# The weight-block sums of a seven-product projection, computed by GpSimd instead of VectorE

## The chip, the cores and the metric

The kernel runs on one core of a Trainium2 chip. A core has five engines that run their own instruction streams and wait for each other through semaphores: TensorE (PE, matrix products; PEld is its weight load), VectorE (DVE, elementwise), ScalarE (ACT, functions, copies and casts), GpSimd (POOL, elementwise, here almost idle) and SyncE (SP, which issues transfers). The metric is the device time of one execution in microseconds; a shorter time is better. Before the change the median of 3 runs is 1056.26 us (1055.57 to 1057.36).

## The reference

One inference step of a decoder trunk of two layers, for a prompt of 512 tokens and 8 sample tokens, 1024 wide. Layer 0 is a recurrent branch beside a state-space branch. Layer 1, where the change lies, is this, cut to what matters:

```python
def layer_c(h, p, s_c, lb, norm_w, w_in, c_norm_w, w_out, ple_w, ple_g):
    u = rmsnorm(h, norm_w) @ w_in
    q, fx, v, gate = jnp.split(u, [HK_C, 2 * HK_C, 2 * HK_C + D_C], axis=-1)
    g = jnp.logaddexp(jnp.log(lb), jnp.log1p(-lb) + jax.nn.log_sigmoid(fx))
    k = (1.0 - lb) * jax.nn.sigmoid(-fx)
    o, new_c = hgrn2_scan(q * DK_C ** -0.5, k, v, g, s_c)      # 16 heads of 128 x 128, by chunks
    o = o * lax.rsqrt(jnp.mean(o * o, axis=-1, keepdims=True) + EPS)
    o = o.reshape(Bsz, L, D_C) * c_norm_w * jax.nn.silu(gate)
    h = h + o.astype(h.dtype) @ w_out
    return per_layer_embed(h, p, ple_w, ple_g), new_c
```

The projection `u` has the four parts q, f (`fx`), v and gate (g), each 1024 x 2048 weights for 16 heads.

## The kernel before, in words

All 520 tokens (512 of the prompt, 8 samples) stay on the chip, features on the partitions, tokens on the free axis. Every float32 weight is loaded raw into `wraw` (two buffers of 128x2048) and split into a rounded part (`whir`, made by ACT) and the rest (`wlor` = raw minus rounded part, made by DVE); a product is then three matmuls, rounded weight by both parts of the activations and the rest by the rounded activations. In layer 1 the splits go through a ring with room for four half-size pieces (128x512) of either part, so a piece can be prepared at most a few products ahead of TensorE.

Layer 1 (`layer1_fast`) works through eight pairs of heads. For the first pair, f and v are plain projections. For the other seven pairs, `strassen` computes f and then v of both heads with seven block products instead of eight. A pair's weight group is cut into four blocks of 128x512: a11 and a12 (the two halves of the 1024 inputs, first head), a21 and a22 (the same, second head); the tokens are cut into two halves of 260. Four sums of weight blocks are needed: s3 = a11 + a21, then a21 = a21 + a22 in place, s2 = a21 + a11, and later a12 = a12 + s2 in place. The seven products take, in the order of the code, a11, s2, s3, a12 as loaded, the new a21, the new a12 and a22, each after its own split (`split_half`). DVE adds the products together from PSUM. s2 and s3 live in two buffers (tag `sgt`); v's s3 takes the buffer of f's s3 and v's s2 that of f's s2, so each can be written only when f's has been used up. Each product is 12 matmuls of 260 columns.

Around them, each pair also runs `decay` (a scan along the prompt per head), `samples` (the 8 samples' states: 30 small DVE updates of 128x128 and 18 scalings on ACT or DVE, and one matmul per head named `os`), and `head`, twice: `A`, `kt`, `kv` on PE, the chunk states S (`l1d`) on DVE, seven matmuls named `o`, the root mean square of the output with its power on POOL (`at__1738<-at__1738,nhalf`, `pow`), and the transpose `ot`.

The order of the work is not the order of the code. A planner (`Plan.order`) takes every recorded operation with its data dependences, a price per operation from a table (`COST`: a DVE `tensor_tensor` of n columns 0.067 + n/960 us, a POOL one 0.21 + n/480 us) and a due time, and plays the five engines through; each engine's instructions are then issued in the sequence that came out, and on the chip each engine keeps to it. A piece of work that the plan thinks ready earlier is therefore put earlier in the stream of every engine that takes part. Operations that may run on ACT or DVE (`copy`, `scaled`) go to the one that is free first in the plan. PE's `os` and `o` blocks are put behind their inputs with a spare of 0.6 us. The plan's prices do not know of one engine's access holding up another's. Nearly all instructions are recorded by `issue`, so they all carry line L520 in the profile and are told apart by their tiles.

Of the kernel before, what the change touches and what calls it, by code (L numbers as in the profile page):

```python
# [21 lines left out]
MUL, ADD, SUB, MAX, MIN = ALU.mult, ALU.add, ALU.subtract, ALU.max, ALU.min  # L22
# [187 lines left out]
class Plan:  # L210
# [31 lines left out]
    @contextmanager  # L242
    def side(self, start=0.0, rate=0.0, pinned=False):

        keep = self.shift, self.rate, self.pinned
        self.shift, self.rate, self.pinned = start, rate, pinned
        yield
        self.shift, self.rate, self.pinned = keep
# [15 lines left out]
    @contextmanager  # L264
    def block(self, main=False):

        self.open = Op(self, self.pos + self.shift, 0)
        self.open.forms["pe"] = [[], 0.0, None]
        self.open.main = main
        self.open.ins, self.open.outs = [], []  # L270
        yield
        op, self.open = self.open, None
        op.forms["pe"][1] /= 2400.0
        self.add(op, op.ins, op.outs)
# [266 lines left out]
def hybrid_decode_step_kernel(ctx: ExitStack, tc: tile.TileContext, I, O, mode="both"):  # L541
# [19 lines left out]
    act, dve, pool, pe, sp = (Engine(plans, k) for k in ("act", "dve", "pool", "pe", "sp"))  # L561
    side, block = (lambda *a, **k: plans[-1].side(*a, **k)), (lambda *a: plans[-1].block(*a))

    def new(pool_, shape, tag, name, bufs=1, dt=F32):
        return plans[-1].tile(pool_, shape, dt, tag, name, bufs, {"psm": PSUM, "psa": PSUM, "drp": DRAM}.get(pool_, SBUF))
# [4 lines left out]
    def mmps(name):  # L570
        return new("psm", [128, 2, 512], "mm", name, 2)

    def grab(name):

        return new("psa", [128, 512], "ax", name)
# [10 lines left out]
    def tt(out, a, b, op, eng=dve):  # L586
        eng.tensor_tensor(out=out, in0=a, in1=b, op=op)
# [13 lines left out]
    def copy(out, in_):  # L601

        plans[-1].record(("act", "copy", (out, in_), {}), ("dve", "tensor_copy", (out, in_), {}))
# [25 lines left out]
    def load_group(g):  # L629
        ap, k0, kk, c, w = groups[g]  # L630
        r = new("wp", [128, 2048], "raw", f"wraw{g}", 2)
        v = r[:, :kk * w].rearrange("p (k c) -> p k c", k=kk)
        with side(*((plans[-1].shift, 0.0, True) if plans[-1].pinned else (-LOAD_AHEAD,))):
            sp.dma_start(out=v, in_=ap[k0 * 128:(k0 + kk) * 128, c:c + w].rearrange("(k p) c -> p k c", p=128))
        raw_of[g] = v
# [9 lines left out]
    def split_half(v):  # L645

        hv, lv = (r.rearrange("p (k c) -> p k c", k=4) for r in ring_space(1))
        with side(-SPLIT_AHEAD):
            act.copy(hv, v)
            tt(lv, v, hv.bitcast(F32), SUB)  # L650
        return hv, lv
# [959 lines left out]
    def layer1_fast():  # L1611
# [93 lines left out]
        def strassen(pr, names):  # L1705

            pss, n = [], 0

            def product(u, x):
                nonlocal n  # L1710

                i = n % 6
                if i % 3 == 2:
                    out = grab(f"sg{pr}_{n}")[:, :HN]
                else:
                    if i < 2:
                        pss[i:] = [mmps(f"sm{pr}_{n}")]
                    out = pss[i % 3][:, i // 3, :HN]
                n += 1
                hw, lw = u  # L1720
                for k in range(4):
                    with block(True):
                        for i, (w, b) in enumerate(((hw, x[0]), (hw, x[1]), (lw, x[0]))):
                            pe.matmul(out, lhsT=w[:, k], rhs=b[:, k], start=(k == 0 and i == 0), stop=(k == 3 and i == 2))
                    plans[-1].pos += 0.334
                return out

            def steps(nm):
                e, e1 = 2 * pr, 2 * pr + 1
                start, done = (start_f, done_f) if nm == "f" else (start_v, done_v)  # L1730
                o0, o1 = start(e), start(e1)
                l0, r0, l1, r1 = o0[:, :HN], o0[:, HN:], o1[:, :HN], o1[:, HN:]
                g = units[sec[f"{nm}{pr}"]][0]
                if g not in raw_of:
                    load_group(g)
                v = raw_of[g]
                a11, a12, a21, a22 = v[:, :4, :128], v[:, 4:, :128], v[:, :4, 128:], v[:, 4:, 128:]
                s2, s3 = (new("cst", [128, N], "sgt", f"{nm}{pr}s{i}", 2)[:, :512].rearrange("p (k c) -> p k c", k=4)
                          for i in range(2))
                w = split_half(a11)  # L1740
                with side(-SPLIT_AHEAD):
                    tt(s3, a11, a21, ADD)
                    tt(a21, a21, a22, ADD)
                    tt(s2, a21, a11, ADD)
                p1 = product(w, x11)
                copy(l0, p1)
                p6 = product(split_half(s2), u2)
                tt(r0, l0, p6, ADD)
                p7 = product(split_half(s3), t3)
                tt(l1, p7, r0, SUB)  # L1750
                w = split_half(a12)
                with side(-SPLIT_AHEAD):
                    tt(a12, a12, s2, ADD)
                p2 = product(w, x21)
                tt(l0, l0, p2, ADD)
                p5 = product(split_half(a21), u1)
                tt(r1, l1, p5, SUB)
                tt(r0, r0, p5, ADD)
                p3 = product(split_half(a12), x22)
                tt(r0, r0, p3, ADD)  # L1760
                done(e)
                p4 = product(split_half(a22), u4)
                tt(l1, l1, p4, ADD)
                done(e1)

            for nm in names:
                steps(nm)
# [497 lines left out]
```

## Time and profile before

| | before |
|---|---|
| median of 3 runs | 1056.26 us |
| the profiled execution's own time | 1052.58 us |
| its span (first to last instruction) | 1050.9 us |
| busy share PE / DVE / ACT / POOL | 97% / 79% / 60% / 13% |
| granted TensorE clock | 0.994 |

The profiled execution lies 3.7 us under the median of the runs. Layer 1's pairs take about 450 us to 950 us of the span. A row of a group gives busy time, mean duration and the idle time before; a row of the timeline gives start, duration, engine and operation, the output tile before the arrow and inputs after it; consecutive DVE instructions overlap a little in the record, so that a 128x512 sum that lasts 0.68 us is followed by the next after 0.60 us.

### The profile page before, as it was taken

How to read it: one execution, taken by the hardware profiler on the slowest of the kernel's cores; microseconds unless marked ns; L12 is line 12 of the kernel's file. 1: busy time of each engine (PE TensorE's matmuls, PEld its weight loads, DVE VectorE, ACT ScalarE, POOL GpSimd, SP SyncE). 2: the span in 40 equal slices, each digit the busy share in tenths (PEclk: the TensorE clock that was granted, in tenths of full speed). 3: DMA queues.
4: the chain of work that ended last, by engine and by line, in shares of the span. 5: the costliest groups of instructions: out<-in, count | busy, mean ns of one | idle time of the engine just before them, and what ended most of it. 6: DMA issues, size and time to landing. Idle time of an engine off the chain costs nothing.

```text
span 1050.9 us, 21517 instructions
## 1 busy us (share of the span) xinstructions
PE 1023.1 (97%) x8427; PEld 1000.0 (95%) x8427; DVE 832.6 (79%) x1705; ACT 630.8 (60%) x1482; POOL 139.4 (13%) x241
## 2 busy tenths in 40 slices
PE   9989899999999999999999999999999999999995
PEld 8989899899999999999999999999999999999995
DVE  6789788998996656697989759698598979868853
ACT  6588876654673222365676726678268685764553
POOL 4635854100000000001000000001000000100000
PEclk9999999999999999999999999999999999999998
DMA  9712254336586223553353433433434443553311
GB/s 285 246 30 92 81 166 141 122 110 191 188 257 213 89 98 117 153 203 90 98 149 109 142 91 108 139 100 113 122 90 139 124 116 111 137 180 121 121 41 45
DMA packets 129957, 138.45 MB, mean 132 GB/s; under 512 B 13704, under 2 KB 111128, under 8 KB 129832
## 3 DMA queue, kind: packets, MB, share of 16 engines
q1 hardware_dynamic: 129464, 136.64, 42.6%
q8 instruction: 68, 1.11, 0.4%
q10 hardware_dynamic: 160, 0.30, 0.1%
q14 instruction: 41, 0.34, 0.1%
q0 software_dynamic: 224, 0.06, 0.0%
HBM read 111.71 MB, written 25.44 MB: 131 GB/s over the span
## 4 chain that ended last, share of the span: by engine, by line
PE 73%; DVE 10%; DMA 6%; ACT 4%; POOL 3%; issue 2%; SPq 0%; POOLq 0%; ACTq 0%; DVEq 0%
PE o L520 10%; PE sm L520 9%; PE q L520 9%; PE pg L520 9%; PE g L520 8%; PE ob L520 4%; PE sg L520 4%; PE xbc L520 2%; PE ax L520 2%; DVE wlo L520 2%; PE oa L520 2%; PE pl L520 2%; PE z L520 1%; DMA smp<-in_state_b_ssm_dram 1%; POOL csm L520 1%
## 5 line engine op out<-in xcount | busy, mean ns | idle before, releaser
L520 ACT CAST whir<-wraw 128x512 fp32r<-128x512 f32 (+1 forms) x121 | 96.3, 798 | 83.9 <-PE o L520 40.6
L520 DVE TENSOR_TENSOR wlor<-wraw,whir 128x512 fp32r<-128x512 f32 (+1 forms) x121 | 109.6, 910 | 12.5 <-ACT whir L520 12.1
L520 ACT CAST whi<-wraw 128x1024 fp32r<-128x1024 f32 (+1 forms) x56 | 57.8, 1032 | 48.6 <-PE ob L520 34.5
L520 POOL TENSOR_TENSOR at__1738<-at__1738,nhalf 128x4 f32<-128x4 f32 (+1 forms) x24 | 22.6, 942 | 461.5 <-DVE at__1738 L520 455.5
L520 DVE TENSOR_TENSOR wlo<-wraw,whi 128x1024 fp32r<-128x1024 f32 (+1 forms) x64 | 77.3, 1208 | 8.0 <-ACT whi L520 7.4
L520 PE MATMUL o<-ohl,whir 128*128 128x260 f32 x512 | 83.0, 284 | 0.0
L520 PEld LDWEIGHTS o<-ohl,whir 128*128 128x128 f32 x512 | 70.0, 188 | 0.9 <-issue 0.6
L520 PE MATMUL g<-xh,whir 128*128 128x260 f32 x256 | 54.6, 294 | 1.1 <-DVE l1a L520 1.1
L520 PE MATMUL q<-xh,whir 128*128 128x260 f32 x256 | 53.2, 289 | 0.0
L520 PE MATMUL q<-xh,wlor 128*128 128x260 f32 x256 | 51.5, 283 | 0.0
L520 PE MATMUL q<-xl,whir 128*128 128x260 f32 x256 | 51.4, 282 | 0.0
L520 PE MATMUL g<-xl,whir 128*128 128x260 f32 x256 | 51.4, 282 | 0.0
L520 PE MATMUL g<-xh,wlor 128*128 128x260 f32 x256 | 51.4, 282 | 0.0
L520 PE MATMUL o<-ohl,wlor 128*128 128x260 f32 x256 | 51.4, 282 | 0.0
L520 DVE TENSOR_TENSOR h<-h,o 128x520 f32<-128x520 f32 x40 | 27.8, 694 | 26.2 <-PE o L520 25.9
L515 ACT ACT_TABLE_LOAD x36 | 46.2, 1283 | 0.6
L520 PE MATMUL sm<-uh,whir 128*128 128x260 f32 x140 | 40.4, 289 | 1.8 <-DVE l1a L520 1.6
L520 PE MATMUL sm<-xh,whir 128*128 128x260 f32 x140 | 41.4, 296 | 0.0
L520 PEld LDWEIGHTS g<-xh,whir 128*128 128x128 f32 x256 | 39.2, 189 | 2.2 <-DVE l1a L520 1.3
L520 PE MATMUL sm<-xh,wlor 128*128 128x260 f32 x140 | 39.6, 283 | 0.3 <-DVE wlor L520 0.3
L520 PE MATMUL xbc<-xnh,whi 128*128 128x260 f32 x192 | 39.7, 289 | 0.0
L520 PE MATMUL sm<-xl,whir 128*128 128x260 f32 x140 | 39.6, 283 | 0.0
(609 smaller groups left out, 3594.2 us busy)
## 6 DMA issues: line engine op xcount, KB each, us to landing
wraw<-in_c_w_in_dram SPq DMA_DIRECT2D x32, 1024.0 KB
wraw<-in_ab_w_in_dram SPq DMA_DIRECT2D x15, 1024.0 KB
wraw<-in_ab_w_out_dram SPq DMA_DIRECT2D x8, 1024.0 KB
wraw<-in_ple_gate_dram SPq DMA_DIRECT2D x8, 1024.0 KB
wraw<-in_c_w_out_dram SPq DMA_DIRECT2D x8, 1024.0 KB
pl<-pl_d SPq DMA_DIRECT2D x2, 2080.0 KB
smp<-in_state_b_ssm_dram SPq DMA_DIRECT2D x8, 512.0 KB
acy<-acsT_d SPq DMA_DIRECT2D x8, 512.0 KB
```

Of the source, the lines that this page charges most:

```text
L515: self.engines["act"].preload_act_table_set(SETS[table])
L520: getattr(f, name)(*a, **k)
```

## The change

All four sums of weight blocks in `strassen` are issued to POOL instead of DVE: 4 in each of 14 sets (f and v of seven pairs), 56 instructions. Nothing else in the text of the kernel is changed.

```diff
                 w = split_half(a11)
                 with side(-SPLIT_AHEAD):
-                    tt(s3, a11, a21, ADD)
-                    tt(a21, a21, a22, ADD)
-                    tt(s2, a21, a11, ADD)
+                    tt(s3, a11, a21, ADD, pool)
+                    tt(a21, a21, a22, ADD, pool)
+                    tt(s2, a21, a11, ADD, pool)
                 p1 = product(w, x11)
...
                 w = split_half(a12)
                 with side(-SPLIT_AHEAD):
-                    tt(a12, a12, s2, ADD)
+                    tt(a12, a12, s2, ADD, pool)
                 p2 = product(w, x21)
```

Since the planner orders by its prices, the whole order from layer 1's first seven-product set on is another one. Three places of it follow.

POOL, from the masks of layer 1 on, first set and beginning of the second (f1s and v1s are the buffers s3 and s2 of the first such pair; rows with - were there before):

```order
 L520 AFFINE_SELECT l1d<-l1d 128x32 x2
-L520 TENSOR_TENSOR at__1738<-at__1738,nhalf 128x4
-L520 TENSOR_TENSOR at__1738<-at__1738,nhalf 16x1
...
+L520 TENSOR_TENSOR f1s_5906<-wraw_5830 128x512
+L520 TENSOR_TENSOR wraw_5830<-wraw_5830 128x4x128
+L520 TENSOR_TENSOR f1s_6021<-wraw_5830 128x512
+L520 TENSOR_TENSOR v1s_6129<-wraw_5964 128x512
+L520 TENSOR_TENSOR wraw_5830<-wraw_5830,f1s_6021 128x4x128
+L520 TENSOR_TENSOR wraw_5964<-wraw_5964 128x4x128
+L520 TENSOR_TENSOR at__1738<-at__1738,nhalf 128x4
+L520 TENSOR_TENSOR v1s_6286<-wraw_5964 128x512
+L520 TENSOR_TENSOR wraw_5964<-wraw_5964,v1s_6286 128x4x128
```

POOL had only the powers here; now v's second sum (v1s_6286, s2) stands behind the power of a head's root mean square.

DVE, where the first pair's sample states end (l1c, l1d) and v's weights begin. Before:

```order
L520 TENSOR_TENSOR wraw_5964<-wraw_5964 128x4x128
L520 SCALAR_TENSOR_TENSOR l1c<-l1d,l1c 128x128
L520 TENSOR_TENSOR v1s_6267<-wraw_5964 128x512
L520 SCALAR_TENSOR_TENSOR l1d<-l1c,l1d 128x128
...
L520 TENSOR_TENSOR wlor_5611<-v1s_6135,whir_5532 128x512
L520 TENSOR_TENSOR wlor_5611<-v1s_6267,whir_5532 128x512
...
L520 TENSOR_TENSOR wraw_5964<-wraw_5964,v1s_6267 128x4x128
L520 SCALAR_TENSOR_TENSOR l1d<-l1c,l1d 128x128
L520 SCALAR_TENSOR_TENSOR l1c<-l1d,l1c 128x128
```

With the change:

```order
L520 TENSOR_TENSOR l1a<-l1a,sm_1_6177 128x260 x2
L520 SCALAR_TENSOR_TENSOR l1d<-l1c,l1d 128x128
L520 TENSOR_SCALAR at__1738<-at__1738 128x4
L520 COPY_PREDICATED l1d<-l1d,A_6058 128x512
L520 SCALAR_TENSOR_TENSOR l1d<-l1c,l1d 128x128
...
L520 TENSOR_TENSOR wlor_5611<-v1s_6129,whir_5532 128x512
...
L520 TENSOR_TENSOR wlor_5611<-v1s_6286,whir_5532 128x512
```

The sums have left, and the last sample updates now stand ahead of the splits of v's sums, where they stood behind them.

PE, the same pair, around `os` and the second head's `o` (sm_6, sm_7, sg_8 are products; sm_7 is v's first, sg_8 v's second, the one that needs s2). Before:

```order
L520 MATMUL sg_8_6335<-uh,wlor_5611 128x260
L520 MATMUL os_6155<-l1d 16x128
L520 MATMUL sg_11_6360<-uh,whir_5439 128x260
...
L520 MATMUL o_6375<-l1b,l1d 128x128 x2
L520 MATMUL o_6375<-l1d,l1a 128x128
```

With the change:

```order
L520 MATMUL sm_6_6248<-uh,wlor_5463 128x260
L520 MATMUL sm_7_6288<-xh_5494,whir_5439 128x260
L520 MATMUL sm_7_6288<-xl_5506,whir_5439 128x260
L520 MATMUL sm_7_6288<-xh_5494,wlor_5463 128x260
L520 MATMUL os_6152<-l1d 16x128
...
L520 MATMUL o_6307<-l1b,l1d 128x128 x2
L520 MATMUL o_6307<-l1d,l1a 128x128
...
L520 MATMUL ot_6329<-ident,l1a 128x128 x4
L520 MATMUL sg_8_6337<-uh,whir_5532 128x260
```

Both `os` and `o` have moved from behind v's second product and beyond into v's first, and v's second product, which stood behind v's first, third and fourth, now follows the first directly.

## The prediction

> **What bounds the kernel now.** I read the page's busy shares first, then a window over layer 1's pairs, where the change lies, then what PE waited for there.
>
> ```profile
> PE 1023.1 (97%) x8427; PEld 1000.0 (95%) x8427; DVE 832.6 (79%) x1705; ACT 630.8 (60%) x1482; POOL 139.4 (13%) x241
> ```
>
> ```profile
> core 0: us, PE busy (x) PEld busy (x) DVE busy (x) ACT busy (x) POOL busy (x), PEclk, DMA share, GB/s
> 450.00:950.00 500.00, 496.42 (x4123) 488.00 (x4122) 411.78 (x946) 335.53 (x834) 27.13 (x32) 1.00 0.42 122
> ```
>
> ```profile
> PE sm L520 <- DVE l1a L520: 1.6, 3, 0.5
> PE g L520 <- DVE l1a L520: 1.1, 1, 1.1
> PE o L520 <- DVE l1d L520: 0.4, 2, 0.2
> PE sm L520 <- DVE wlor L520: 0.3, 1, 0.3
> ```
>
> TensorE is the bound: of 500 us it is idle for 500 - 496.4 = 3.6 us. DVE is the second engine, 411.8 of 500 us, 82%. The waits are those of PE between 446 and 960 us (us in total, times, longest), and they add up to 3.4 us, all on DVE. The change takes work off the engine that PE waits for, but those 3.4 us are all that it can win. What it can lose is any moment at which PE waits for a weight or a state that now comes later.
>
> **What is removed.** DVE did 56 sums of 128x512:
>
> ```profile
> L520 DVE TENSOR_TENSOR wraw<-wraw 128x512 f32<-128x512 f32 x14 | 9.6, 683 | 0.0
> ```
>
> This group is one of the four kinds, 14 instructions; the other kinds have the same shape. They overlap the next instruction a little, so one costs DVE 0.60 us from start to start:
>
> ```profile
> 503.69 0.68 DVE L520 TENSOR_TENSOR v1s<-wraw 128x512 f32<-128x512 f32 x1
> ...
> 507.02 0.68 DVE L520 TENSOR_TENSOR wraw<-wraw,f1s 128x512 f32<-128x512 f32 x1
> ...
> 514.21 0.68 DVE L520 TENSOR_TENSOR wraw<-wraw 128x512 f32<-128x512 f32 x1
> 514.81 0.34 DVE L520 SCALAR_TENSOR_TENSOR l1c<-l1d,l1c 128x128 f32<-128x128 f32 x1
> 515.07 0.68 DVE L520 TENSOR_TENSOR v1s<-wraw 128x512 f32<-128x512 f32 x1
> ...
> 519.50 0.68 DVE L520 TENSOR_TENSOR wraw<-wraw,v1s 128x512 f32<-128x512 f32 x1
> 520.10 0.34 DVE L520 SCALAR_TENSOR_TENSOR l1d<-l1c,l1d 128x128 f32<-128x128 f32 x1
> 520.36 0.34 DVE L520 SCALAR_TENSOR_TENSOR l1c<-l1d,l1c 128x128 f32<-128x128 f32 x1
> ```
>
> That is 56 x 0.60 = 33.6 us off DVE, all of it beside running matmuls. At the end it is worth what of the 3.4 us goes. Three of the waits (0.5 us each, 1.6 in all) sit where PE comes back to the PSUM tile of a product; the new order puts another product between there. The 1.1 us wait lies in a stretch of crowded DVE work. I take -2.0 us, bounds 0 and -3.4.
>
> **What a sum costs on POOL.** No POOL sum of 512 columns is in the trace. The nearest rows:
>
> ```profile
> L520 POOL TENSOR_TENSOR dtt<-dtt,hb 128x80 f32<-128x80 f32 x1 | 0.4, 358 | 0.0
> L520 POOL TENSOR_TENSOR csm<-csm,pt 128x32 f32<-128x32 f32 x2 | 0.5, 240 | 0.1
> L520 POOL MEMSET l1d<- 128x512 f32 x3 | 1.5, 538 | 28.2 <-DVE ul L520 28.2
> L520 POOL TENSOR_TENSOR at__1738<-at__1738,nhalf 128x4 f32<-128x4 f32 x16 | 17.6, 1099 | 297.7 <-DVE at__1738 L520 291.7 <-ACT dtt L520 6.0
> ```
>
> Two sums with two inputs give a slope of (358 - 240) / 48 = 2.46 ns a column, so 358 + 432 x 2.46 = 1.42 us for 512. Below, the fill of 512 columns, which reads nothing, takes 0.54 us. Above, a wait for DVE can come on top (next part). I take 1.4 us, from the two rows of the same operation. POOL then gets 56 x 1.4 = 78 us in 450, so it is no bound, and most sums have time: f's first three can start when the weights have landed, well before f's first product. The plan counts 0.21 + 512/480 = 1.28 us.
>
> The Trainium skill, GPSIMD Engine Reference, section 3.1, gives 4497 ns for this sum at 2048 columns, which in proportion is an estimate of 1.12 us for 512; its section 4.1 advises against elementwise sums on this engine for being about twice as slow as on VectorE. By 1.12 us a sum would end earlier than the plan counts, and the loss below would be about 2 us smaller.
>
> **What a POOL instruction does to DVE.** The rows that decide are in layer 0, where POOL masks 128x1024 tiles:
>
> ```profile
> 225.07 1.23 DVE L520 TENSOR_TENSOR wlo<-wraw,whi 128x1024 fp32r<-128x1024 f32 x1
> 226.21 1.58 DVE L520 SCALAR_TENSOR_TENSOR xa<-sga,xa 128x520 f32<-128x520 f32 x1
> ...
> 225.37 1.88 POOL L520 TENSOR_SCALAR_AFFINE_SELECT wsl<-acy 128x1024 f32<-128x1024 f32 x1 [18.92 <-PE yd L520]
> ```
>
> ```profile
> 205.51 1.48 DVE L520 TENSOR_TENSOR wsl<-wsl,at__1738 128x512 f32<-128x512 f32 x1
> ...
> 205.35 1.09 POOL L520 TENSOR_SCALAR_AFFINE_SELECT wsl<-acy 128x1024 f32<-128x1024 f32 x1 [7.30 <-PE yd L520]
> ```
>
> ```profile
> L520 POOL TENSOR_SCALAR_AFFINE_SELECT wsl<-acy x8: 1088/1092/1890, 147.4 to 225.4; 128x1024 f32<-128x1024 f32 x8
> L520 DVE TENSOR_TENSOR wsl<-wsl,at__1738 x8: 674/683/1480, 173.0 to 233.6; 128x512 f32<-128x512 f32 x8
> ```
>
> The last two rows have minimum, median and maximum. A mask takes 1.09 us alone; at 225.37 it took 1.88, 0.8 longer, until DVE's `wlo` was done. The DVE instruction behind it, with two SBUF inputs, then lasted 1.58 us and ended when the mask did; the one at 205.51 lasted 1.48 instead of 0.68 and also ended with the mask. So each can hold up the other. It is not always so:
>
> ```profile
> 197.36 0.67 DVE L520 TENSOR_TENSOR acy<-acy,yo 128x512 f32<-128x512 f32 x1
> ...
> 196.96 1.09 POOL L520 TENSOR_SCALAR_AFFINE_SELECT wsl<-acy 128x1024 f32<-128x1024 f32 x1 [2.24 <-PE yo L520]
> ```
>
> ```profile
> 521.03 0.68 DVE L520 TENSOR_TENSOR wlor<-wraw,whir 128x512 fp32r<-128x512 f32 x1
> ...
> 520.93 1.03 POOL L520 TENSOR_TENSOR at__1738<-at__1738,nhalf 128x4 f32<-128x4 f32 x1 [40.38 <-DVE at__1738 L520]
> ```
>
> A DVE instruction with an input in PSUM (`yo`) was not held, nor was `wlor` beside a POOL power over 4 columns. The new sums stream 512 columns from two inputs and are nearest to the mask. A hold is 0.8 us beside a mask of 1.09, so up to 0.8 x 1.4 / 1.09 = 1.0 us beside a sum; about six in ten of DVE's time here goes to instructions with two SBUF inputs (`wlor`, the sample updates, the scan), so I take 0.6 us for each sum, bounds 0 and 1.4. Then 56 x 0.6 = 33.6 us come back: DVE's load is what it was.
>
> The Trainium skill, SBUF — State Buffer, section "Who interferes with whom", says that a DVE instruction with two SBUF inputs and a GpSimd instruction that reads SBUF take turns on one port pair, the second waiting for the whole of the first. The masks agree (1.48 for 0.68 us); the power does not (`wlor` 0.68 us beside it).
>
> **Where it reaches PE.** The plan counts DVE as 33.6 us freer and has put `os` and `o` ahead on PE in nearly every pair, as the change's listing shows for the first.
>
> ```profile
> 516.45 0.28 PE L520 MATMUL sm<-xh,wlor 128*128 128x260 f32 x1
> ...
> 522.83 0.39 PE L520 MATMUL os<-l1d 128*16 128x128 f32 x2
> ```
>
> `os` ran at 522.83, 2.1 us after its last input (l1c, 520.36 + 0.34). Its new place is behind the third matmul of v's first product, which ran at 516.45, so it now comes at about 516.6. Ahead of that last input DVE has lost five sums since 500 us (3.0 us), two splits each of v's sums and blocks have gone behind it (4 x 0.60 = 2.4 us), and one 0.7 us masked copy has come in front. Without holds the input is ready at 520.7 - 3.0 - 2.4 + 0.7 = 516.0, 0.6 us early. With four POOL sums in that stretch, each holding DVE 0.6, it is ready at 518.4, 1.8 us late. PE cannot pass over `os`; the products behind it wait, and whatever waits there also delays the splits that feed on freed ring space. Then v's s2: POOL does it behind the power (1.1 us), itself behind DVE's square sum, and its cast and split must be done before v's second product, which now follows the first. There 0.1 us (1.4 against 1.28) and a turn behind DVE of up to 0.8 come on top, partly in the same wait.
>
> One wait of this kind per pair, between 0 and 1.8 us: I take 0.95, so seven pairs give 6.6 us. Bounds 0 and 7 x (1.8 + 0.9) = 19.
>
> **Sum.** -2.0 + 6.6 = +4.6 us on the profiled 1052.6, so 1057.2; the runs' median lies 3.7 us higher, so 1056.26 + 4.6 = 1060.9 us, +0.4%.
>
> **Rivals.** *Faster*: POOL's sums do not hold DVE, as the power does not; then DVE really is 33.6 us freer, the plan holds, and the waits on DVE go: -2.0 to -3.4, so 1053.5 us. For it speaks that the masks are another operation than the sums; against it, that two of the quoted masks held DVE for 0.8 us. It decides where the hold per sum is under about 0.2 us (four of them then fit into the 0.6 us of room). *Same*: holds as forecast, but in the many pairs where DVE drains its backlog before v starts only 0.3 us reach PE, 7 x 0.3 = 2.1, against the 2.0 won: 1056.4. DVE's 88 idle us speak for it. *Much slower*: every sum holds DVE for its whole 1.4 us, net 56 x 0.8 = 45 us on an engine with 88 to spare, which crowds the f and v stretches: 19 us less 2 won, 1073. *POOL the bound*: 56 x (1.4 + 0.8) = 123 us of 450 says no. That the sums stay on DVE is excluded by the listing.
>
> **Chances.** Forecast 40%, much slower 10%, same 22%, faster 28%. A measurement here can tell 0.2%, 2.1 us, from no change. The forecast's own range is 1058 to 1067. To leave out no more than 2 in 10 the range takes in most of the faster case and the lower part of the much slower one: 1052.5 to 1070. Faster 0.28, same 0.22, slower 0.50.
>
> **What would show it.** Right: POOL sums of 1.2 to 2.2 us, DVE instructions with two SBUF inputs stretched by 0.5 to 1.0 us beside them (`wlor` of 512 columns above 0.70 on average), DVE's busy time in the pairs within 10 us of 412, PE idle up by some 5 us there, with waits of `os`, `o` or `sg` on DVE or ACT. Wrong: `wlor` at 0.68 and DVE at 380 (no hold); PE waiting on `whir` for `a12`'s sum (POOL's lateness, not DVE's); or a time outside the range because the new order itself makes or removes waits that have nothing to do with POOL, which this argument takes for small.

## The result, and the profile after

| | before | after |
|---|---|---|
| median of the runs on one chip | 1056.81 us (4 runs, 1055.57 to 1058.14) | 1066.17 us (4 runs, 1063.49 to 1066.92) |
| ratio, 95% interval | | 1.0081 [1.0060, 1.0101] |
| the profiled execution's own time | 1052.58 us | 1063.49 us |
| its span | 1050.9 us | 1061.7 us |
| granted TensorE clock | 0.994 | 0.991 |

The change makes the kernel slower by 0.8%, 9.4 us between the medians. The forecast was slower by 4.6 us, to 1060.9; the direction holds, the size is half of what came. First the page's busy times, then layer 1's pairs, which now reach to 960 us (before, the window ended at 950), then what PE waited for between 446 and 970 us:

```profile
PE 1025.7 (97%) x8427; PEld 1001.1 (94%) x8427; DVE 833.8 (79%) x1664; ACT 627.0 (59%) x1465; POOL 220.6 (21%) x297
```

```profile
450.00:960.00 510.00, 500.40 (x4125) 490.09 (x4124) 412.73 (x903) 331.21 (x816) 108.12 (x88) 1.00 0.41 119
```

```profile
PE sm L520 <- DVE l1b L520: 4.9, 3, 1.8
PE sm L520 <- DVE l1a L520: 2.8, 6, 0.5
PE q L520 <- DVE wlor L520: 0.7, 1, 0.7
PE os L520 <- DVE l1d L520: 0.4, 1, 0.4
PE sm L520 <- DVE wlor L520: 0.3, 1, 0.3
```

56 instructions have left DVE, and it is as busy as it was: 412.7 us in this window against 411.8 in that of before. PE is idle for 510 - 500.4 = 9.6 us instead of 3.6, and all its waits end with a DVE instruction, 9.1 us in all. More than half of that is in three waits for `l1b`.

The work went to POOL, and a part of it came back to DVE as longer instructions. This is one of the four kinds of sums on POOL (minimum, median and maximum in ns), and then three groups of DVE, after and before:

```profile
L520 POOL TENSOR_TENSOR wraw<-wraw x14: 1262/1292/1614, 487.2 to 910.6; 128x512 f32<-128x512 f32 x14
```

```profile
L520 DVE SCALAR_TENSOR_TENSOR l1c<-l1d,l1c 128x128 f32<-128x128 f32 x64 | 34.6, 554 | 0.0
L520 DVE TENSOR_SCALAR dtt<-l1a,lbt 128x8 f32<-128x8 f32 x32 | 14.5, 481 | 0.6 <-ACT l1a L520 0.6
L520 DVE TENSOR_TENSOR wlor<-wraw,whir 128x512 fp32r<-128x512 f32 x70 | 47.7, 682 | 7.9 <-ACT whir L520 7.8
```

```profile
L520 DVE SCALAR_TENSOR_TENSOR l1c<-l1d,l1c 128x128 f32<-128x128 f32 x64 | 21.1, 344 | 0.0
L520 DVE TENSOR_SCALAR dtt<-l1a,lbt 128x8 f32<-128x8 f32 x32 | 7.4, 265 | 0.6 <-ACT l1a L520 0.6
L520 DVE TENSOR_TENSOR wlor<-wraw,whir 128x512 fp32r<-128x512 f32 x70 | 47.3, 684 | 6.8 <-ACT whir L520 6.7
```

The sample updates `l1c` went from 344 to 554 ns on average and the small `dtt` from 265 to 481; `wlor` did not change. Taking each DVE instruction that ran beside one of the 56 sums, and subtracting the median duration of the same instruction before, gives 37.1 us in all, 0.66 us for each sum. Instructions that overlap in the record are each counted in this, so it is rather too much: DVE's busy time on the page is 833.8 us here and 801.2 in experiment 3, which has the same DVE instructions in the same order and nearly no holds, 32.6 us less. Either way, about as much has come back as the 33.6 us that were taken off DVE.

One of the holds and where it ends, from the second of the seven pairs:

```profile
562.75 1.33 POOL L520 TENSOR_TENSOR v2s<-wraw 128x512 f32<-128x512 f32 x1 [16.77 <-DVE wlor L520]
```

```profile
562.59 0.35 DVE L520 SCALAR_TENSOR_TENSOR l1d<-l1c,l1d 128x128 f32<-128x128 f32 x1
562.85 1.65 DVE L520 SCALAR_TENSOR_TENSOR l1c<-l1d,l1c 128x128 f32<-128x128 f32 x2
...
565.74 0.68 DVE L520 SCALAR_TENSOR_TENSOR l1b<-l1b,g 128x520 f32<-128x520 f32 x1
```

```profile
564.40 0.28 PE L520 MATMUL sm<-xh,wlor 128*128 128x260 f32 x1
566.47 0.39 PE L520 MATMUL sm<-uh,whir 128*128 128x260 f32 x1 [1.79 <-DVE l1b L520]
```

POOL's sum (v's s3) starts at 562.75 and DVE's next sample update 0.1 us later. The two updates take 1.65 us instead of 0.6, and end at 564.50, shortly after the sum (564.08). Five short updates stand behind them, then `l1b<-l1b,g`, the last reader of the PSUM tile of the gate product. f's second product is to be written there, and PE waits for it: 2.07 us from one matmul's start to the next, where 0.12 us is usual. (Matmul records overlap, so the 1.79 in the row is less than what is lost.)

One part of the profiled execution's loss is not a wait. Right behind this place the granted TensorE clock (the column after POOL's) was 0.50 for 3.41 us, which costs 1.7 us; the longest `sm` matmuls take 420 ns there, where 283 is the median:

```profile
567.51:570.92 3.41, 3.41 (x18) 3.41 (x17) 3.20 (x7) 0.63 (x1) 2.50 (x2) 0.50 0.44 156
```

The trace of before has no such stretch in layer 1's pairs.

### The profile page after: what moved, and what is told of

It is laid out like the page before. It is cut to its first block, busy times and chain, and to the rows that moved or that the text cites. A ratio compares the mean times of both kernels' runs of the same rounds, so it can differ in the third digit from the quotient of the medians.

```text
span 1061.7 us, 21537 instructions
## 1 busy us (share of the span) xinstructions
PE 1025.7 (97%) x8427; PEld 1001.1 (94%) x8427; DVE 833.8 (79%) x1664; ACT 627.0 (59%) x1465; POOL 220.6 (21%) x297
## 5 line engine op out<-in xcount | busy, mean ns | idle before, releaser
L520 PEld LDWEIGHTS q<-xh,wlor 128*128 128x128 f32 x256 | 39.4, 188 | 1.3 <-DVE wlor L520 0.9
L520 PE MATMUL sm<-ul,whir 128*128 128x260 f32 x140 | 39.9, 285 | 0.0
```

Source lines behind the costliest of these rows:

```text
L520: getattr(f, name)(*a, **k)
```

## The experiments

Twelve kernels. Where operations carry L521 or L522, the kernel has one or two lines more ahead of them. Besides the ratio to the kernel before, a second measure is used, because the part of the execution before layer 1's pairs differs by some us between executions of the same instructions (the first `sm` matmul ran at 506.7 us in the change and at 511.1 in a kernel with the same order). The **stretch of the products** is the time from the first to the last start of a `sm` matmul. For the change it is read from these two rows, 926.4 - 506.7 = 419.7 us:

```profile
L520 PE MATMUL sm<-xh,whir x140: 278/283/420, 506.7 to 924.7; 128*128 128x260 f32 x140
L520 PE MATMUL sm<-uh,wlor x140: 277/282/420, 508.5 to 926.4; 128*128 128x260 f32 x140
```

The 1.7 us of the slower clock are in it. The stretch comes from one execution of each kernel, and is compared between kernels of the same order; between different orders it also contains what else the plan has put in between. "Held" is DVE's lost time beside the sums, worked out as above from the longer durations. For the fills it depends on which neighbours are counted: with every DVE instruction that overlaps one, experiments 3 and 5 come to 2.7 and 2.9 us instead of the 1.4 and 0.4 of the table.

| kernel | order | ratio to before, 95% | stretch | held |
|---|---|---|---|---|
| before | before | 1 | 412.4 | 0 |
| sums issued to POOL | before | 1.0132 [1.0086, 1.0178] | 424.7 | 30.4 |
| the same, fill and power for sums | before | 0.9985 [0.9971, 0.9998] | 411.3 | 0.4 |
| the change | after | 1.0081 [1.0060, 1.0101] | 419.7 | 37.1 |
| sums issued to DVE | after | 1.0049 [1.0029, 1.0069] | 416.7 | 0 |
| fill and power for all sums | after | 1.0000 [0.9983, 1.0017] | 409.5 | 1.4 |
| fill and power for v's s3 alone | after | 1.0027 [1.0009, 1.0044] | 413.7 | 29.9 |
| fill and power for all but v's s3 | after | 1.0027 [1.0012, 1.0042] | 412.3 | 7.4 |
| s3 and s2 computed twice | after | 1.0258 [1.0223, 1.0292] | 436.3 | 54.7 |
| copies for sums | after | 1.0009 [0.9994, 1.0024] | 410.1 | 7.9 |
| plan counts a hold of 0.66 us | new | 1.0119 [1.0074, 1.0164] | 424.2 | 29.2 |
| v's s3 planned on DVE | new | 1.0113 [1.0084, 1.0143] | 425.8 | 34.0 |
| only f's s3, a21, s2 on POOL | new | 1.0134 [1.0103, 1.0165] | 424.9 | 7.8 |
| the same, fill and power for sums | that | 1.0104 [1.0072, 1.0135] | 420.1 | 0.4 |

The theories at the start: (1) POOL's sums hold DVE, so that DVE is later than the order assumes, and PE pays where it has no room; (2) POOL's sums are late, since one takes twice as long as on DVE; (3) the new order is worse by itself.

### 1. The order of before, the sums issued to POOL

All sums pass through a helper `wsum`; the plan takes one as DVE's, and where the instruction is issued it goes to POOL.

```diff
+        def wsum(out, a, b):
+            tt(out, a, b, ADD, dve)
+            plans[-1].ops[-1].run = "pool"
...
-            f = self.engines[op.taken]
+            f = self.engines[getattr(op, "run", op.taken)]
```

> The order of the kernel before (the plan prices the sums as DVE's), but each of the 56 sums is issued to POOL at the same place. Theory 1, holds against the plan (POOL sums hold DVE for about 0.66 us each, 37 us in all, and the change's plan counts them as free): DVE's load is what this order was planned for (33.6 us of sums gone, about 37 us of holds come), so the time is that of before, 1054 to 1060 us. Rival 2, lateness of the sums themselves (1.32 us or more on POOL, with a semaphore to wait for, against 0.68 on DVE): these are all here, so 1062 us or more. Rival 3, the new order alone is worse: as before, 1053 to 1058 us. Total stretch of DVE instructions beside the sums by theory 1: 25 to 45 us.

Measured: 1067.72 us, ratio 1.0132 [1.0086, 1.0178]. Theory 1 as stated here missed: it took an order that plans for a sum on DVE to have room for a hold of about the same size. DVE's load is no larger than before, and the order is the old one, and yet this is no faster than the change: a loss of this size needs no new order. PE's waits:

```profile
PE sm L520 <- DVE l1a L520: 9.0, 10, 2.0
PE sm L520 <- DVE l1b L520: 2.6, 2, 1.3
PE g L520 <- DVE l1a L520: 1.2, 1, 1.2
```

The longest of them, followed back on DVE and POOL:

```profile
648.98 1.34 POOL L520 TENSOR_TENSOR wraw<-wraw 128x512 f32<-128x512 f32 x1
649.09 1.78 DVE L520 TENSOR_TENSOR wlor<-wraw,whir 128x512 fp32r<-128x512 f32 x1
650.40 1.65 POOL L520 TENSOR_TENSOR v3s<-wraw 128x512 f32<-128x512 f32 x1
650.80 0.41 DVE L520 TENSOR_TENSOR l1a<-l1a,sm 128x260 f32<-128x260 f32 x1
651.13 1.06 DVE L520 SCALAR_TENSOR_TENSOR l1c<-l1d,l1c 128x128 f32<-128x128 f32 x1
...
654.45 0.41 DVE L520 TENSOR_TENSOR l1a<-l1a,sm 128x260 f32<-128x260 f32 x1
...
655.00 0.36 PE L520 MATMUL sm<-uh,whir 128*128 128x260 f32 x1 [1.96 <-DVE l1a L520]
```

Two sums hold two DVE instructions, by 1.1 and 0.7 us, together 1.8. The `l1a<-l1a,sm` that frees the PSUM tile is the seventh DVE instruction behind them, and PE stands for 1.96 us. Held time that falls just ahead of such an instruction arrives at PE undiminished; that as much work was removed somewhere else on DVE does not pay for it.

### 2. The order of the change, the sums issued to DVE

The reverse: planned on POOL, issued to DVE (`tt(out, a, b, ADD, pool)`, `run = "dve"`).

> The order of the changed kernel (the plan prices the sums as POOL's), but each sum is issued to DVE at the same place of the sequence. No POOL instruction holds DVE, and the sums take 0.68 us; but DVE has 33.6 us of work that this order does not count. Theory 1 (DVE is late against the order by what the plan does not count, whether holds or sums): slower than before like the change, 1062 to 1068 us. Rival 2 (lateness of the sums on POOL): gone, 1054 to 1058 us. Rival 3 (the new order alone): 1064 to 1068 us.

Measured: 1061.39 us, ratio 1.0049 [1.0029, 1.0069], just under the range of theory 1. Nothing is held here; DVE has 33.6 us of work that the order does not know of, and that alone costs 416.7 - 409.5 = 7.2 us in the stretch (against experiment 3; 5.2 us by the ratios). The wait at 566.47 us of the change is here:

```profile
566.95 0.39 PE L520 MATMUL sm<-uh,whir 128*128 128x260 f32 x1 [1.36 <-DVE l1b L520]
```

### 3. The order and the engines of the change, without streaming

POOL fills the tile and raises four columns to a power instead of the sum; it is busy at least as long, and everything waits for it as before. The sums are left out.

```diff
+            plans[-1].ops[-1].instead = [("memset", (out, 1.0), {}),
+                ("tensor_tensor", (), {"out": out[:, 0, :4], "in0": ones[:, :4],
+                                       "in1": a[:, 0, :4], "op": ALU.pow})]
...
             calls, _, func = op.forms[op.taken]
+            calls = getattr(op, "instead", calls)
```

> The changed kernel's order and engines; each POOL sum is replaced by a fill of the same 128x512 tile (0.54 us, reads nothing) and a power over 4 of its columns (about 1.0 us, held nobody before): together at least as long as a sum (1.32 us) and waited for in the same way, but without two streams read over 512 columns. The four sums are not computed, so what f and v become is not the model's. Theory 1 (holds): DVE is really as free as the plan counts, total stretch under 8 us, time 1051 to 1057 us, that is 9 to 15 us under the change. Rival 2 (lateness of the sums): 1063 to 1068 us, as the change or worse. Rival 3 (the new order alone): 1064 to 1067 us.

Measured: 1056.78 us, ratio 1.0000 [0.9983, 1.0017]. Held: 1.4 us. PE's waits in the pairs:

```profile
PE sm L521 <- DVE l1b L521: 2.0, 3, 0.8
PE q L521 <- DVE wlor L521: 0.7, 1, 0.7
PE os L521 <- DVE l1d L521: 0.6, 1, 0.6
```

```profile
568.52 0.38 PE L521 MATMUL sm<-uh,whir 128*128 128x260 f32 x1 [0.75 <-DVE l1b L521]
```

Order, engines and POOL's busy time are those of the change, and the loss is gone: the stretch is 409.5 us against 419.7, 10.2 us less. In this trace no part of the stretch runs at half clock, so 1.7 of the 10.2 us are the slower clock of the change's profiled execution, and 8.5 are what PE loses by the holds; the ratios of the runs give 8.6 us. Whether the slower clock is itself brought by the holds is not shown. Theories 2 and 3 fall for this change. The same wait is 0.75 us without a hold, 1.36 with one more sum of 0.60 us on DVE (0.61 more), and 1.79 with a hold of 1.05 us (1.04 more): at this place PE pays for DVE's delay one to one. But the kernel is not faster than before either, although DVE is 33.6 us freer.

### 4. The plan counts the hold

The planner adds 0.66 us to DVE for each sum on POOL.

```diff
                 fin = clk[e] = t + c
+                if getattr(op, "hold", 0):
+                    clk["dve"] = max(clk["dve"], t) + op.hold
```

> The changed kernel, sums on POOL, with one line in the planner: whenever it places one of these sums on POOL it also takes DVE for 0.66 us, the mean stretch found in the changed kernel's trace. Theory 1: the order then fits what the chip does, so most of the loss is gone: 1053 to 1059 us, with the total stretch still 25 to 45 us. Rival 2 (lateness of the sums on POOL): they are as late as in the change, 1062 us or more. Rival 3 says nothing of this order.

Measured: 1068.48 us, ratio 1.0119 [1.0074, 1.0164]; missed. With the load right on average the order is no better. PE now waits at other places, most of all at `l1a` (4.3 us) and `o` (1.6). Experiment 1 suggests why an average would not do: the hold is 0 or up to 1.1 us, on whatever instruction stands beside the sum. How much of this loss is held time and how much the new order was not separated.

### 5. The order of before, without streaming

Experiment 1 with the fill and the power of experiment 3; the sums are left out.

> The order of before, as in the run with that order, but where GpSimd did a sum it now fills the same 128x512 tile and raises four columns to a power, so it is busy as long and the later instructions wait for it as they did, without reading 512 columns; the sums are left out. Theory (a GpSimd instruction that reads 512 columns holds DVE's next instruction, and this order has no room for 1 us at the places where PE comes back to a PSUM tile): the 11 us of that order go, PE's waits on l1a fall from 9.0 us to under 3, 1053 to 1057 us. Since nothing holds DVE and 33.6 us are off it, it also measures the gain that the prediction put at 2.0 us: 1054.7 if it is there. Rival (the sum is late on GpSimd, where it takes twice as long as on DVE, and all that waits for it is late in an order that was made for DVE): GpSimd is busy as long, so 1062 to 1068.

Measured: 1054.21 us, ratio 0.9985 [0.9971, 0.9998]. The 11 us of experiment 1 are gone here too (stretch 411.3 against 424.7, and neither trace has a part of it at half clock), with POOL as busy and the order that was made for DVE: lateness of the sums does not matter in this order either. This is also what 33.6 us less on DVE are worth if nobody is held: 0.15%, 1.6 us, between 0.2 and 3.1. Of the 3.4 us of waits before, only the 0.4 us at `o` have gone; the others are still there, within 0.01 us. First PE's waits in this kernel, then the DVE instruction behind one of the three of 0.5 us, in the kernel before and in this one:

```profile
PE sm L521 <- DVE l1a L521: 1.6, 3, 0.5
PE g L521 <- DVE l1a L521: 1.2, 1, 1.2
PE sm L521 <- DVE wlor L521: 0.3, 1, 0.3
```

```profile
518.55 0.42 DVE L520 TENSOR_TENSOR l1a<-l1a,sm 128x260 f32<-128x260 f32 x1 [0.44 <-PE sm L520]
```

```profile
519.75 0.43 DVE L521 TENSOR_TENSOR l1a<-l1a,sm 128x260 f32<-128x260 f32 x1 [0.44 <-PE sm L521]
```

DVE was not busy when PE waited for it. It had been idle for 0.44 us, waiting for PE's own product; PE then waited for the addition of that product. This is the time of one trip from PE to DVE and back, and the 33.6 us taken off DVE did not shorten it. At the other two of these waits DVE had been idle as well, for 0.95 and 0.44 us. The wait of 1.1 us at `g` is another case: DVE had hardly been idle ahead of it, two of the sums that ran there are gone, and it is as long as it was; what sets it was not found.

### 6. and 7. Seven of the sums left out, and these seven alone

In the second, fourth and sixth pair v's s3 ran ahead of the long wait shown above. In one kernel only v's s3 (one of the four kinds for v, seven of 56 sums) becomes the fill and the power and is left out; in the other all the rest is, and left out.

```diff
             tt(out, a, b, ADD, pool)
+            if which == "vs3":           # in the other: !=
+                plans[-1].ops[-1].instead = [fill, power]
```

> The change, but of its 56 sums only the seven that are v's first (s3) are replaced by the fill and the power over four columns, and left out. They are those that ran beside the 1.65 us scan step of DVE at 562.8 us, and again in every other pair, just ahead of a 1.4 to 1.8 us idle time of PE. Theory (the place of a hold decides): these three idle times fall to under 0.8 us each, PE's waits on l1b from 4.9 to 2.0 us or less, and the run is 2 to 4 us faster than the change, 1062 to 1064. Rival (only the sum of DVE's lost time counts, wherever it falls): seven of 56 sums are an eighth of the 9.4 us, 1.2 us, so about 1065, with idle times that shrink everywhere a little.

> The reverse of the run with seven sums left out: of the change's 56 sums only these seven, v's first (s3), are computed on GpSimd; the other 49 are replaced by the fill and the power over four columns, and left out. Theory (place): the 1.4 to 1.8 us idle times of PE at f's second product in every other pair come back with these seven alone, and the time is 4 to 6 us above the run that left out all 56, at 1060.5 to 1063; DVE time lost beside the sums about 7 us. Rival (the total counts): 7 of 37 us, a fifth of 9.4, so 1058.5; or the holds only hurt together, one after another, so 1056 to 1058.

Measured, without the seven: 1058.88 us, 1.0027 [1.0009, 1.0044], faster than either expectation; the stretch is 413.7 us, 6.0 less than the change, of which 1.7 are the change's slower clock. (The profiled execution was the slowest of its ten, 1065.69 us; most of the excess lies ahead of the products, which start at 513.5 us.) The three long waits are 0.76, 0.59 and 0.75 us, and the waits on `l1b` 2.1 us in all. An eighth of the sums, with a fifth of the held time (7.2 of 37.1 us), makes half of the loss (4.3 of 8.5): the place decides. With the seven alone: 1059.76 us, 1.0027 [1.0012, 1.0042], below the range, and at another place than expected:

```profile
PE os L521 <- DVE l1d L521: 3.2, 3, 1.5
PE sm L521 <- DVE l1b L521: 2.3, 3, 0.8
```

```profile
561.64 1.32 POOL L521 TENSOR_TENSOR v2s<-wraw 128x512 f32<-128x512 f32 x1 [14.55 <-DVE wlor L521]
561.74 1.38 DVE L521 SCALAR_TENSOR_TENSOR l1c<-l1d,l1c 128x128 f32<-128x128 f32 x1
...
564.05 0.38 PE L521 MATMUL os<-l1d 128*16 128x128 f32 x2 [1.48 <-DVE l1d L521]
```

The same sum holds the same update, but DVE is earlier here, since the other sums hold it no longer; PE arrives at `os` while DVE is still working on its inputs, waits there 1.5 us, and the second product behind it finds its tile no later than in experiment 3 (0.76 us). So the seven cost 2.8 us alone and 4.3 with the others, the others 4.2 alone: 7.0 of 8.5 us if each is taken by itself. The rest, 1.5 us, would be there only because held time adds up on DVE; it rests on one execution of each kernel.

### 8. s3 and s2 computed twice

First the difference into the same tile, then the sum; the output is the same.

```diff
+            if which[1:] in ("s3", "s2"):
+                plans[-1].ops[-1].instead = [(a - b into out), (a + b into out)]
```

> The change, with s3 and s2 computed twice on GpSimd (first the difference into the same tile, then the sum; the output is the same): 28 more instructions that stream 512 columns. Theory: each holds DVE like the others, 0.66 us, so the DVE time lost beside them goes from 37 to 50 to 57 us, and the time rises in proportion or more than that, to 1070 to 1078. Rival (the 9 us come from a few places that have already taken all that one sum can do): 1065 to 1068, with holds of 50 us and more.

Measured: 1083.12 us, ratio 1.0258 [1.0223, 1.0292], above the range. Held: 54.7 us, 17.6 more than in the change, and the stretch is 16.6 us longer. Here 10.2 us of the stretch ran at half clock, in the change 3.4, so 3.4 of the 16.6 us are the clock's. Without it the first 37 us of held time cost 8.5, the next 17.6 about 13. `os` now waits as well:

```profile
PE sm L521 <- DVE l1b L521: 8.6, 3, 2.9
PE os L521 <- DVE l1d L521: 6.4, 7, 1.4
PE sm L521 <- DVE l1a L521: 5.5, 9, 0.8
```

The doubled sums also end later; how much of these 13 us is that was not separated.

### 9. A copy instead of the sum

POOL copies the first input, 128x512; the sums are left out.

```diff
+            plans[-1].ops[-1].instead = [("tensor_copy", (out, a), {})]
```

> The change, with each GpSimd sum replaced by a copy of its first input, 128x512: one input is read in place of two, and the sums are left out. Theory (whatever reads 512 columns on GpSimd takes turns with DVE): DVE instructions are still stretched beside the copies, in proportion to a copy's duration, 15 to 37 us in all, and the time is 1059 to 1066. Rival (two inputs are needed): under 5 us of stretching and 1055 to 1058.5, as with the fill.

Measured: 1056.93 us, ratio 1.0009 [0.9994, 1.0024], held 7.9 us: the time is in the range of the rival, the held time between the two expectations. One input does hold DVE, but the copy is half as long as a sum, and the hold lasts only as long as the copy:

```profile
562.09 0.67 POOL L521 COPY v2s<-wraw 128x512 f32<-128x512 f32 x1 [16.69 <-DVE wlor L521]
562.21 0.70 DVE L521 SCALAR_TENSOR_TENSOR l1c<-l1d,l1c 128x128 f32<-128x128 f32 x1
```

The update ends 0.15 us after the copy (562.91 and 562.76); beside the sum of experiment 7 it ended 0.16 us after the sum (563.12 and 562.96). Here it lost 0.36 us, there 1.04.

### 10. to 12. Fewer sums on POOL, with orders of their own

Two complete kernels: v's s3 planned and run on DVE, the other 49 sums on POOL; and only f's first three sums on POOL.

```diff
-            tt(out, a, b, ADD, pool)
+            if which == "vs3":                        # second kernel: which not in ("fs3", "fa21", "fs2")
+                tt(out, a, b, ADD)
+            else:
+                tt(out, a, b, ADD, pool)
```

> Everything is computed: v's first sum (s3) goes to DVE in the plan as well, the other 49 sums go to GpSimd as in the change, and the order is worked out anew. By the place theory the idle times at f's second product go if the new order leaves the sums where they are, and 1058 to 1061 follows; but a new order puts other sums beside other instructions that PE waits for, as it did where the plan counted the hold, and then it is 1061 to 1068. I put three in ten on the first. Rival (the total counts): 30 us of hold for 37, so 1064.8.

> Everything is computed: only f's first three sums (s3, a21, s2) go to GpSimd, in the plan as well, and the other 35 stay on DVE. In every other pair of the change these three ran long before their product and held DVE for nothing, in the others they held it 2.5 us together. Place theory: the few places decide, and v's sums, which were the costly ones, are off GpSimd, so 1055 to 1060, with 8 to 15 us of hold. The gain cannot be over about 1.5 us, what the run with the order of before and no hold gained. Rival (the total counts): 10 us of hold, 12.6 us off DVE, so 1057 to 1060 from the same numbers; this run sizes the cost rather than tells the two apart.

Measured: 1069.17 us, 1.0113 [1.0084, 1.0143], above both of its ranges and nearer the less welcome one; and 1069.79 us, 1.0134 [1.0103, 1.0165], a clear miss: 7.8 us of held time cannot cost that much. In its trace DVE stands before v's first sum of the last pair, because its weights have not landed, and PE stands behind it:

```profile
906.51 0.69 DVE L521 TENSOR_TENSOR v7s<-wraw 128x512 f32<-128x512 f32 x1 [5.40 <-DMA wraw<-in_c_w_in_dram]
```

```profile
910.05 0.59 PE L521 MATMUL sm<-uh,whir 128*128 128x260 f32 x1 [3.56 <-DVE l1b L521]
```

So a new question: is this order bad without any hold? The last kernel keeps the order and puts the fill and the power in the place of its 21 sums, which are left out.

> The order of the run in which only f's first three sums are planned on GpSimd, with those 21 sums replaced by the fill and the power over four columns, and left out. In that run 7.8 us of DVE time were lost beside the sums, and DVE stood 5.4 us before v's first sum of the last pair, waiting for its weights, with PE idle for 3.6 us behind it. Theory (the holds cost by their place): then the time falls by several us, to 1058 to 1063, as it did when the change's own holds were taken out. Rival (this new order is bad by itself, holds or not: what was planned with one set of times meets a DVE queue that waits for weights): 1066 to 1069, the 5.4 us stay.

Measured: 1066.88 us, ratio 1.0104 [1.0072, 1.0135]. The rival is right: most of this loss is the order's own, and the row is still there:

```profile
904.95 0.69 DVE L521 TENSOR_TENSOR v7s<-wraw 128x512 f32<-128x512 f32 x1 [4.92 <-DMA wraw<-in_c_w_in_dram]
```

(The stretches differ by 4.8 us, but in the kernel with the sums 6.8 us ran at half clock, from 909.22 us on, which makes 3.4 of them.) Theory 3 is therefore a real danger of such a change, which can cost 10 us by itself; the order of the change happens to be one that costs nothing that the runs can tell (experiment 3). No kernel that computes everything was faster than the one before.

## Why the prediction was right or wrong

**DVE as second engine, its load after the change: right.** The prediction let 33.6 us leave and 33.6 come back, and asked for a load within 10 us of 412; it is 412.7, and 33 to 37 us came back.

**The price of a sum on POOL: right.** Taken 1.4 us from two narrower sums, bounds 0.54 and more; the median of the quoted 14 is 1.29, that of all 56 is 1.32, none was under 1.26, and the longest, beside DVE, was 2.26. The figure of the Trainium skill (GPSIMD Engine Reference, section 3.1), in proportion an estimate of 1.12 us, is lower than any of them.

**The hold: right in size, wrong in who is held.** Taken 0.6 us for each sum, with bounds 0 and 1.4; 0.66 on average, between 0 and 1.1. The masks of layer 0 were the right rows to choose, and the power the wrong ones: experiment 3 puts the power beside the same DVE instructions and holds 1.4 us in all, all of it beside the fills. But the sign that was named, `wlor` above 0.70 us, did not come in the change (0.682). In the order of the change the sums run beside the sample updates and the `dtt`; in the order of before they met `wlor` (1.78 us in experiment 1). One reading of the masks was off: the two DVE instructions did not end with the mask but 0.54 and 0.55 us after it (226.21 + 1.58 against 225.37 + 1.88, 205.51 + 1.48 against 205.35 + 1.09). That the rule of the Trainium skill (SBUF — State Buffer, "Who interferes with whom") makes the second wait for the whole of the first agrees nearly: an update of 0.34 us ends 0.15 us after a copy and 0.16 after a sum, the 512 columns of 0.68 us end 0.55 us after the mask, so all but 0.13 to 0.19 us of the second instruction comes behind the first.

**The gain of 2.0 us: the step that failed.** "The change takes work off the engine that PE waits for, but those 3.4 us are all that it can win", and -2.0 was taken. With nothing held, the old order wins 1.6 us at best estimate (0.2 to 3.1), but the waits on which the 2.0 was counted, the three of 0.5 us and the one of 1.1, are all still there (experiment 5); only 0.4 us at `o` went. The three are trips from PE to DVE and back. The trace of before showed it, in the row at 518.55: DVE's idle time of 0.44 us, ended by PE. The prediction read which engine PE waited for and did not read what that engine had waited for. Its other ground, "the new order puts another product between there", is right for the three waits: with nothing held, the new order has none on `l1a` (experiment 3). But it has waits of its own in their place, 2.0 us on `l1b`, 0.7 and 0.6, together 3.3 against 3.4, and the time is that of before (1.0000, with an uncertainty of 0.0017, 1.8 us). With the holds the waits on `l1a` are back, 2.8 us against 1.6.

**Where it reaches PE: the mechanism right, the place wrong.** "One wait of this kind per pair", at `os`, `o` or v's second product. `os` waited 0.4 us in all. DVE was mostly in time for `os`; what it was late with stood behind, at the additions and copies that free PSUM tiles: f's second product in every other pair (4.9 us), and products behind `l1a` in the others. With fewer holds (experiment 7) the wait is at `os`, as predicted; with more (experiment 8) it is at both.

**Its size: too small.** 0.95 us a pair, 6.6 in all, bounds 0 and 19; against the same order without holds it is 10.2 us in the stretch, 8.5 without the slower clock, 1.2 a pair. By the runs' ratios it is 0.81% against 0.00%, 8.6 us, with an uncertainty of about 2.8 from the two intervals. So of the 4.8 us between forecast and result about 2 lie in the gain that was not there and about 2 to 3 in this term, and the slower clock is nowhere in the sum. The 0.95 was a value picked about halfway between 0 and 1.8, so that it came this near is in part luck. What the sum did not have: at the PSUM tile of 566.47 us a hold is paid one to one, where the prediction counted with 0.6 us of room at `os`; and in the order of before two holds stand just ahead of one such tile (experiment 1).

**The rivals.** *Faster* falls, since the holds exist; and where nothing is held, 1.6 us are won in the old order (0.2 to 3.1) and none in the new one (experiments 5 and 3). *Same* needed 0.3 us per pair and the 2 us won; neither came. *Much slower* supposed a hold of the whole sum for each; on average it was half that, and where the sums are made longer (experiment 8) the time goes past 1073. *POOL the bound*: POOL is busy for 108 us of 510; no. That the new order might itself change the time was called small; for this change it was (1.0000), but experiment 12 shows 1.04% from the order of a smaller change.

## What to carry to other kernels

Before a wait on an engine is credited to its load, read what that engine was waiting for just before: if it was idle, and waiting for the one that now waits, moving work away wins nothing. Work that goes to an engine whose instructions hold those of the first is moved only in the listing (here 33.6 us went and about as much came back): price the hold by the longer instruction's duration, and look for the next place behind it at which the bottleneck engine needs a tile freed. Where a planner makes a new order of each change, the order is a change of its own: run it once with the suspected cost taken out before blaming that cost.

## What the runs showed of the hardware

- A GpSimd instruction that streams 512 columns held DVE instructions until it ended, with two inputs (sum, 1.26 us and more, DVE up to 1.1 us late) as with one (copy, 0.67 us, DVE 0.36 late). A fill of 512 columns and a power over four columns, together rather longer than a sum, held them for 1 to 3 us in 56 pairs, by the count. The power held none of them. The fill let two-input updates pass, but not the `tensor_scalar` instructions `sqt<-sqt,l1d` of 128x128: one that started at 503.43 us in experiment 3, beside a fill from 503.36 to 503.98, took 0.63 us instead of 0.28.
- Not only DVE instructions with two tensors from SBUF were held: `dtt<-l1a,lbt`, a `tensor_scalar` of 128x8 with one tensor input, went from a median of 0.28 us to as much as 1.26 us.

```profile
L520 DVE TENSOR_SCALAR dtt<-l1a,lbt x32: 215/280/1255, 464.7 to 920.9; 128x8 f32<-128x8 f32 x32
```

The Trainium skill (SBUF — State Buffer, "Who interferes with whom") lists `tensor_scalar` among the operations that can enter a mode with both ports, and this row agrees.
- What a hold costs TensorE is set by its place and by the others around it: the same seven sums cost 4.3 us among the others and 2.8 alone.
- Granted clock: within layer 1's pairs, half clock for 3.4 or 6.8 us at a time is seen only in traces with waits of PE of 1.8 us and more, each time during such a wait or about 1 us after it (the change at 567.51 us, experiment 8 at 569.59 and 712.95, the kernel of experiments 10 to 12 with f's first three sums at 909.22). It does not follow every such wait: not the change's at 837.80 us, as long as that at 566.47, nor the one of 1.96 us in experiment 1.
